# Two of the three gathered tiles of a PEER expert layer: rows of V gathered by token and summed by VectorE in PSUM, in place of TensorE products

## The chip, the cores and the metric

One core of one Trainium2 chip. The metric is device time in microseconds of one execution; the median of three runs of the kernel before is 3828.0 us (3827.8 to 3831.39).

## What is computed

One layer over 1024 tokens of width 1024: an attention and a long-convolution branch, then a PEER expert layer. For each token and each of 8 heads, product keys pick 16 of 16384 experts; expert e is one neuron with a row of U and a row of V. Only this last part bears on the change (cut from the reference):

```
best, pos = lax.top_k(cand, PEER_TOPK)
eidx = jnp.take_along_axis(cidx, pos, axis=-1)
g = jax.nn.softmax(best, axis=-1)
a = jnp.einsum('chkd,cd->chk', u_tab[eidx], xc)
wgt = (jax.nn.gelu(a.astype(jnp.float32)) * g).astype(xc.dtype)
return jnp.einsum('chk,chkd->cd', wgt, v_tab[eidx])
```

So every token has 128 experts, 128 weights, and its output is the weighted sum of 128 rows of V, 4 KB each.

## The kernel before

The 1024 tokens are 8 tiles of 128. Tiles 0 to 4 (`DT = 5`) go through **dense()**: it runs over all 128 blocks of 128 experts, whatever was picked. For each block it loads uT (`ur`) and V (`vr`), splits both into a high and a low part (`split`, lines 89 and 90: ScalarE copies, VectorE or, for half of the V blocks, GpSimd subtracts), forms the activations of 640 tokens with 48 matmuls of 320 columns (`mm3`, lines 84 to 86; gelu on ScalarE, line 1022), multiplies them with the gate weights on VectorE (line 982) and splits them again. After each chunk of four blocks (`CH = 4`), `products` multiplies them with V, 12 matmuls of 512 columns for each of 10 results, and VectorE adds each result to an accumulator in SBUF (line 1004). The PSUM pool of these results has five banks.

Tiles 5 to 7 (`E`) are **gathered**. `usweep` fetches, for each of the 128 experts of a token, the rows of U with a token per partition (an indirect DMA issued by GpSimd, line 886), and VectorE multiplies each with the token's vector and sums (line 887, with a second short instruction that reads the accumulator). `vsweep` fetches rows of V in another layout: an expert per partition (line 911, indices `eT`, transposed), one gather for 32 experts of 4 tokens at a time, as the order of the tokens wants it. TensorE sums over the partitions: eight matmuls of 32x512 for four gathers (line 915) with weights laid out on diagonals (`wdz`, lines 905 and 906), accumulated in PSUM (`acc`, two banks). All eight wait for the fourth gather. Both layouts fetch the same bytes: 128 gathers of 512 KB for a tile. In the profile each of these float32 matmuls is two records, so one step of four gathers is 16.

The buffers: `row`, 7 of 4 KB a partition (`RW`), shared by usweep's and vsweep's gathers; `vg`, 2 (`VB`), of which a step of vsweep takes one; and `h2`, one, in which usweep holds the tile's tokens.

What sets the order: `weave` runs dense() and takes steps of `background()` between its steps. background() runs usweep of tile 5; then usweep of tile 6 in turn with vsweep of tile 5; usweep of tile 7 in turn with vsweep of tile 6; then vsweep of tile 7. Each step is four gathers with what consumes them. From this a scheduler makes the order on each engine. Each engine then works in its order: an instruction that waits holds back all that stand behind it.

Of the kernel before, what the change touches and what calls it, by code (L numbers as in the profile page):

```python
# [10 lines left out]
F32 = mybir.dt.float32  # L11
# [4 lines left out]
OP = mybir.AluOpType  # L16
# [5 lines left out]
D = 1024  # L22
# [31 lines left out]
RW = 7  # L54
VB = 2
# [6 lines left out]
GB4, MGB4, OA4, OB4 = 2, 2, 1, 3  # L62
ND, DC = 2, 23
LR = 3
BGR = 1.3
DT = 5


def body(tc, d, out, dbg=None):
# [11 lines left out]
    V, S, G, PE, SY = nc.vector, nc.scalar, nc.gpsimd, nc.tensor, nc.sync  # L81
# [10 lines left out]
    with es:  # L92
# [194 lines left out]
        with ExitStack() as st:  # L287
# [15 lines left out]
            with ExitStack() as s2:  # L303
                p = pool("xp", 1, stack=s2)
# [111 lines left out]
            p = pool("zp", 2, stack=sz_, side="right")  # L416
# [164 lines left out]
            p = pool("zg", 2, stack=st, side="right")  # L581
# [314 lines left out]
        def vsweep(i, tops, ws, p, gp, ms, ap, res, wdz):  # L896
            w, eT = ws[i], tops[i][2]
            pt = ms.tile([128, 512], F32, name="ms")
            PE.transpose(pt[:, :128], w, ident)
            acc = ap.tile([128, 2, 512], F32, name="acc")  # L900
            pv = pt[:, :128].rearrange("p (c t) -> p c t", c=4)
            wT = res.tile([128, 4, 32], F32, name="wT", bufs=1)
            V.tensor_copy(wT, pv)
            for th in range(8):
                V.memset(wdz, 0.0)
                V.tensor_copy(wdz[:, :, th * 4:128:33], wT[:, :, th * 4:th * 4 + 4])
                for tm in range(4):
                    tl = th * 4 + tm
                    vgs = [gp.tile([128, D], F32, name="row", bufs=RW) if c else p.tile([128, D], F32, name="vg", bufs=VB) for c in range(4)]
                    for c in range(4):  # L910
                        G.indirect_dma_start(out=vgs[c], out_offset=None, in_=d["v"], in_offset=bass.IndirectOffsetOnAxis(ap=eT[:, c * 32 + tl:c * 32 + tl + 1], axis=0))  # L911
                    lead = None
                    for h in range(2):
                        for c in (3, 0, 1, 2):
                            mm = PE.matmul(acc[c * 32:c * 32 + 32, h, :], wdz[:, c, tm * 32:tm * 32 + 32], vgs[c][:, h * 512:(h + 1) * 512],  # L915
                                           start=tl == 0, stop=tl == 31, tile_position=(0, c * 32))
                            if lead is None:
                                lead = mm
                            else:
                                tc.add_manual_dep(mm.ins, lead.ins.name, mybir.DependencyInfo(mybir.DependencyClass.NoSync, mybir.DependencyReason.DATA), reason="behind the last gather")  # L920
                    yield 1
            gt = [gp.tile([128, D], F32, name="row", bufs=RW) for _ in range(4)]
            gates(gt)
            final(i, acc.rearrange("p a b -> p (a b)"), gt[2], gt[3], gt, p)


        def gbuild(i, i1T, i2T, gT, p, ms, on_act, gb, ob=False):
            for g in range(4):
# [121 lines left out]
        def gates(gt):  # L1050
            SY.dma_start(gt[0], modd[3:4, :].to_broadcast([128, D]))
            SY.dma_start(gt[1], d["fin_g"].to_broadcast([128, D]))
# [41 lines left out]
        E = list(range(DT, 8))  # L1094
        tops, ws = {}, {}
        with ExitStack() as sg:
# [19 lines left out]
            with ExitStack() as sk:  # L1116
                tkv = pool("tkv", 1, stack=sk)
                ra, rb = [], []
                sa_.close()
                sr_ = ExitStack()  # L1120
                rps = pool("rps", RB, PSUM, stack=sr_)
                rwp = pool("rw", 2, stack=sr_)
                for _ in rest(0, 4, rps, rwp, tkv, ra, hq):
                    pass
                v16, i16, hTh, hTl = ra
                ms = pool("ms", 1, PSUM, stack=sg, side="right")
                def weights_of(tiles, v16, i16, pools, on_act, gb):
                    bp, mg, tk, st_ = pools
                    for i in tiles:
                        for _ in topk(i, v16[:, i % 4], i16[:, i % 4], tk, bp, ms, True):  # L1130
                            pass
                        if i == DT - 1:
                            st_.close()
                        yield 1
                        yield from gbuild(i, *tops[i], bp, mg, on_act, gb, i < 4)

                def pools(stack, i, mgb):
                    st_ = stack.enter_context(ExitStack())
                    return (pool(f"gb{i}", 1, stack=stack, side="right"), pool(f"mg{i}", mgb, PSUM, stack=stack, side="right"),
                            pool(f"tk{i}", 1, stack=st_, side="right"), st_)  # L1140

                with ExitStack() as sb:
                    pl = pools(sb, 0, MGB)
                    rg = rest(4, 4, rps, rwp, tkv, rb, keep=(hTh[:, :, 512:], hTl[:, :, 512:]))
                    for _ in range(RB0):
                        next(rg)
                    for _ in weave(rg, weights_of(DD[:4], v16, i16, pl, OA, GB), RBR):
                        pass
                    pl[3].close()
                sr_.close()  # L1150
                v16, i16, _, _ = rb
                with ExitStack() as sb:
                    for _ in weights_of(DD[4:], v16, i16, pools(sb, 4, MGB4), OA4, GB4):
                        pass
                gp = pool("gp", 1, stack=sg, side="right")
                sl = ExitStack()
                tk = pool("tk2", 1, stack=sl, side="right")
                us = [usweep(i, tops, ws, gp, None, res) for i in E]

                def background():  # L1160
                    def tk_(i):
                        return topk(i, v16[:, i % 4], i16[:, i % 4], tk, res, ms, False)

                    yield from tk_(E[0])
                    for i in E[1:]:
                        yield from alternate(tk_(i), first(us[0], 24))
                    sl.close()
                    vp = pool("vp", 1, stack=sg, side="right")
                    ap = pool("ap", 1, PSUM, stack=sg, side="right")
                    wdz = vp.tile([128, 4, 128], F32, name="wdz")  # L1170
                    vs = [vsweep(i, tops, ws, vp, gp, ms, ap, res, wdz) for i in E]
                    yield from us[0]
                    for j in range(len(E) - 1):
                        yield from alternate(us[j + 1], vs[j])
                    yield from vs[-1]

                left = weave(dense(hTh, hTl, gp), background(), BGR)
                for _ in left:
                    pass
# [101 lines left out]
```

## Time and profile before

| | |
|---|---|
| median of three runs | 3828.0 us |
| the profiled execution | 3827.45 us |
| its span, first to last instruction | 3825.7 us |
| PE busy | 3526.5 us (92%) |
| VectorE (DVE) busy | 2449.8 us (64%) |
| ScalarE (ACT) busy | 1449.6 us (38%) |
| GpSimd (POOL) busy | 1672.5 us (44%) |
| mean granted TensorE clock | 0.958 of 2.4 GHz |

Times in the trace are microseconds from the span's start. The dense part begins at about 1700 us. Gathers of U run from 1865 to 3259 us, gathers of V from 1947 to 3540 us. VectorE's last step for tile 5 (line 1058) is at 2725.9 us, for tile 7 at 3554.1 us. A busy engine isn't always the one that holds the others up; the waits tell that, and PE's matmuls overlap in their records, so that a PE at 100% may still wait a little.

### The profile page before, as it was taken

Reading aid. Unit: us, or ns where it says so; the run is one execution under the profiler, and the core shown is the slowest. Engines: PE = TensorE matmul, PEld = TensorE weight load, DVE = VectorE, ACT = ScalarE, POOL = GpSimd, SP = SyncE. Lnnn points to the kernel's source line nnn. Section 1 sums busy time; section 2 is a strip of 40 time slices with the busy share of each in tenths; the row PEclk is TensorE's granted clock in tenths of the full one; section 3 lists DMA queues with packets and bytes.
Section 4 is the critical chain, followed back from the end, with each engine's and each line's share of the span. In section 5 each row is a group of like instructions: output and inputs, shape, how many; then the busy total and the mean of one; then the engine's idle time right before and its main releaser. Section 6 shows DMA issues by size and latency. Waiting matters only on the chain. (4 is left out here: it accounts for less than half of the span.)

```text
span 3825.7 us, 56007 instructions
## 1 busy us (share of the span) xinstructions
PE 3526.5 (92%) x21140; PEld 2963.8 (77%) x21140; DVE 2449.8 (64%) x5095; ACT 1449.6 (38%) x2966; POOL 1672.5 (44%) x1360
## 2 busy tenths in 40 slices
PE   5898998789989786989798999999999999999998
PEld 3787987567878686878688878888887888777897
DVE  4656544664446999999888766666556666433445
ACT  5543422446564278976312221212221222212222
POOL 0232143221321664123677666666565666556110
PEclk6999999999999897999899999999999999999999
DMA  4554355763322334443688899999999998989532
GB/s 161 184 157 155 121 204 197 273 218 101 108 83 67 119 141 173 156 164 130 214 311 304 303 335 328 336 343 327 331 326 337 335 343 314 353 318 333 172 108 98
DMA packets 334251, 868.48 MB, mean 227 GB/s; under 512 B 31778, under 2 KB 145378, under 8 KB 324765
## 3 DMA queue, kind: packets, MB, share of 16 engines
q0 software_dynamic: 123904, 453.04, 32.9%
q1 hardware_dynamic: 210076, 411.87, 31.4%
q8 instruction: 166, 2.72, 0.3%
q14 instruction: 105, 0.85, 0.1%
HBM read 777.63 MB, written 87.18 MB: 226 GB/s over the span
## 5 line engine op out<-in xcount | busy, mean ns | idle before, releaser
L84 PE MATMUL mm<-h2Th,uh 128*128 128x320 f32 x2048 | 641.0, 313 | 29.1 <-ACT uh L89 18.0
L86 PE MATMUL mm<-h2Th,ul 128*128 128x320 f32 x2048 | 638.2, 313 | 7.5 <-DVE ul L90 7.4
L85 PE MATMUL mm<-h2Tl,uh 128*128 128x320 f32 x2048 | 640.0, 313 | 0.0
L887 DVE SCALAR_TENSOR_TENSOR row<-row,h 128x1024 f32<-128x1024 f32 x384 | 493.9, 1306 | 153.2 <-DMA row<-in_u,ei 130.0
L886 POOL DMA_INDIRECT row<-in_u,ei x384 | 472.7, 1231 | 180.1 <-issue 85.9
L84 PE MATMUL mm<-vh,wh 128*128 128x512 f32 x1280 | 495.0, 396 | 25.5 <-DVE acc L1004 15.1
L85 PE MATMUL mm<-vl,wh 128*128 128x512 f32 x1280 | 502.0, 393 | 2.9 <-POOL vl L90 2.8
L86 PE MATMUL mm<-vh,wl 128*128 128x512 f32 x1280 | 497.2, 394 | 5.4 <-DVE wl L90 5.4
L911 POOL DMA_INDIRECT row<-in_v,eT x288 | 347.1, 1205 | 343.2 <-PE acc L915 179.7
L84 PEld LDWEIGHTS mm<-h2Th,uh 128*128 128x128 f32 x2048 | 389.3, 190 | 49.9 <-ACT uh L89 19.0
L86 PEld LDWEIGHTS mm<-h2Th,ul 128*128 128x128 f32 x2048 | 388.3, 190 | 22.9 <-issue 12.6
L85 PEld LDWEIGHTS mm<-h2Tl,uh 128*128 128x128 f32 x2048 | 389.1, 190 | 18.2 <-issue 16.8
L1004 DVE TENSOR_TENSOR acc<-acc,mm 128x512 f32<-128x512 f32 x322 | 211.9, 683 | 275.3 <-PE mm L86 275.1
L89 ACT CAST vh<-vr 128x1024 fp32r<-128x1024 f32 x133 | 139.3, 1048 | 474.1 <-PE mm L86 299.9
L84 PEld LDWEIGHTS mm<-vh,wh 128*128 128x128 f32 x1280 | 242.4, 190 | 89.8 <-DVE acc L1004 19.7
L86 PEld LDWEIGHTS mm<-vh,wl 128*128 128x128 f32 x1280 | 242.0, 189 | 72.8 <-issue 15.9
L85 PEld LDWEIGHTS mm<-vl,wh 128*128 128x128 f32 x1280 | 242.6, 190 | 60.3 <-issue 7.5
L90 POOL TENSOR_TENSOR vl<-vr,vh 128x1024 fp32r<-128x1024 f32 x67 | 167.8, 2505 | 251.3 <-ACT vh L89 250.7
L90 DVE TENSOR_TENSOR ul<-ur,uh 128x1024 fp32r<-128x1024 f32 (+1 forms) x130 | 169.3, 1302 | 162.7 <-ACT uh L89 161.3
L1022 ACT ACTIVATE ga<-mm 128x320 f32<-128x320 f32 x256 | 110.2, 436 | 421.2 <-PE mm L86 298.8
L89 ACT CAST uh<-ur 128x1024 fp32r<-128x1024 f32 (+1 forms) x130 | 137.8, 1060 | 268.7 <-DMA ur<-in_uT 177.8
L89 ACT CAST wh<-ga 128x640 fp32r<-128x640 f32 (+2 forms) x136 | 94.7, 696 | 362.8 <-DVE ga L982 189.3
(363 smaller groups left out, 7934.6 us busy)
## 6 DMA issues: line engine op xcount, KB each, us to landing
vr<-in_v SPq DMA_DIRECT2D x133, 512.0 KB
ur<-in_uT SPq DMA_DIRECT2D x128, 512.0 KB
gd<-gst SPq DMA_DIRECT2D x40, 1024.0 KB
gt<-gd SPq DMA_DIRECT2D x32, 1024.0 KB
wt<-in_ada_w SPq DMA_DIRECT2D x12, 2048.0 KB
cfr<-in_cf POOLq DMA_DIRECT2D x32, 512.0 KB, 5.2
mt<-in_cf POOLq DMA_DIRECT2D x16, 1024.0 KB, 6.4
mt<-in_ci POOLq DMA_DIRECT2D x16, 1024.0 KB, 7.7
```

The source lines that it names most:

```text
L84: PE.matmul(ps, ah, bh, start=start, stop=False)
L85: PE.matmul(ps, ah, bl, start=False, stop=False)
L86: PE.matmul(ps, al, bh, start=False, stop=stop)
L89: S.copy(hi, src)
L90: (eng or V).tensor_tensor(lo, src, hi.bitcast(F32), OP.subtract)
L886: G.indirect_dma_start(out=ug, out_offset=None, in_=d["u"], in_offset=bass.IndirectOffsetOnAxis(ap=ei[:, s_:s_ + 1], axis=0))
L887: V.scalar_tensor_tensor(ug, ug, 1.0, h2, OP.mult, OP.mult, accum_out=a[:, s_:s_ + 1])
L911: G.indirect_dma_start(out=vgs[c], out_offset=None, in_=d["v"], in_offset=bass.IndirectOffsetOnAxis(ap=eT[:, c * 32 + tl:c * 32 + tl + 1], ...
L1004: V.tensor_tensor(acc[:, i, h, :], acc[:, i, h, :], po, OP.add)
L1022: S.activation(ga[:, ts_], pa[:, :NS], AF.Gelu_apprx_tanh)
```

## The change

For tiles 6 and 7 (`VD`), a new function `vrows` takes the place of `vsweep`. It gathers rows of V with a token per partition, as usweep does for U: gather s fetches expert s of all 128 tokens (indices `ei`, as they are). VectorE multiplies the gathered tile by the column s of the weights and adds it to `acc`, one instruction for each gather (the first writes, the other 127 add in place). `acc` is the same two banks of PSUM; the last step (line 1058 and those behind it) stays. Tile 5 keeps vsweep.

The buffers are others: of three gathers in a row the second takes `row` in tile 6 and the one `h2` in tile 7 (usweep is through by then), the first and the third take `vg`.

```diff
+VD = (6, 7)
...
+        def vrows(i, tops, ws, p, gp, ap):
+
+            w, ei = ws[i], tops[i][1]
+            acc = ap.tile([128, 2, 512], F32, name="acc").rearrange("p a b -> p (a b)")
+            for s_ in range(128):
+                row = gp.tile([128, D], F32, name="h2" if i == 7 else "row", bufs=1 if i == 7 else RW) if s_ % 3 == 1 else p.tile([128, D], F32, name="vg", bufs=VB)
+                G.indirect_dma_start(out=row, out_offset=None, in_=d["v"], in_offset=bass.IndirectOffsetOnAxis(ap=ei[:, s_:s_ + 1], axis=0))
+                if s_ == 0:
+                    V.tensor_scalar(acc, row, w[:, 0:1], None, OP.mult)
+                else:
+                    V.scalar_tensor_tensor(acc, row, w[:, s_:s_ + 1], acc, OP.mult, OP.add)
+                if s_ % 4 == 3:
+                    yield 1
+            gt = [gp.tile([128, D], F32, name="row", bufs=RW) for _ in range(4)]
+            gates(gt)
+            final(i, acc, gt[2], gt[3], gt, p)
...
-                    vs = [vsweep(i, tops, ws, vp, gp, ms, ap, res, wdz) for i in E]
+                    vs = [vsweep(i, tops, ws, vp, gp, ms, ap, res, wdz) for i in E if i not in VD]
+                    vs += [vrows(i, tops, ws, vp, gp, ap) for i in VD]
```

Up to the first sum of tile 6 the order on VectorE is the same as before. Behind it the scheduler sets every engine's order anew. Line numbers of the changed kernel are higher: by 1 up to `vsweep`, by 18 behind `vrows` (L1004 is L1022 there, L982 is L1000); the gather is L933, the sum L937.

On VectorE, in the products of a chunk while tile 7's rows of U (L887, reading `h`, the tile's tokens) are gathered; before:

```order
L1004 TENSOR_TENSOR acc<-acc,mm 128x512 x6
L887 SCALAR_TENSOR_TENSOR row,a<-row,h_21926 128x1024
L1004 TENSOR_TENSOR acc<-acc,mm 128x512
L887 SCALAR_TENSOR_TENSOR row,a<-row,h_21926 128x1024
L1004 TENSOR_TENSOR acc<-acc,mm 128x512
L887 SCALAR_TENSOR_TENSOR row,a<-row,h_21926 128x1024
L1004 TENSOR_TENSOR acc<-acc,mm 128x512
L887 SCALAR_TENSOR_TENSOR row,a<-row,h_21926 128x1024
L1004 TENSOR_TENSOR acc<-acc,mm 128x512
L887 SCALAR_TENSOR_TENSOR row,a<-row,h_21926 128x1024 x2
L90 TENSOR_TENSOR ul<-ur,uh 128x1024
```

The same place in the changed kernel, with tile 6's sums of V among them (L888 is the old L887):

```order
L1022 TENSOR_TENSOR acc<-acc,mm 128x512
L937 SCALAR_TENSOR_TENSOR acc<-vg,gw_18487,acc 128x1024
L1022 TENSOR_TENSOR acc<-acc,mm 128x512
L937 SCALAR_TENSOR_TENSOR acc<-vg,gw_18487,acc 128x1024
L937 SCALAR_TENSOR_TENSOR acc<-row,gw_18487,acc 128x1024
L888 SCALAR_TENSOR_TENSOR row,a<-row,h_21926 128x1024
L1022 TENSOR_TENSOR acc<-acc,mm 128x512
L888 SCALAR_TENSOR_TENSOR row,a<-row,h_21926 128x1024
L1022 TENSOR_TENSOR acc<-acc,mm 128x512
L888 SCALAR_TENSOR_TENSOR row,a<-row,h_21926 128x1024 x2
L1022 TENSOR_TENSOR acc<-acc,mm 128x512
L937 SCALAR_TENSOR_TENSOR acc<-vg,gw_18487,acc 128x1024 x2
```

Between two emptyings of a bank there stand now up to three sums, of two kinds, where one stood.

On VectorE, in the products of a chunk after the last row of U; before:

```order
L905 MEMSET wdz 128x512
L1004 TENSOR_TENSOR acc<-acc,mm 128x512
L906 COPY wdz<-wT 128x4x4
L1004 TENSOR_TENSOR acc<-acc,mm 128x512 x6
L90 TENSOR_TENSOR wl<-ga_31002,wh 128x128
L1004 TENSOR_TENSOR acc<-acc,mm 128x512
```

And in the changed kernel, in tile 7's sums (the `h_` are the one buffer h2):

```order
L1022 TENSOR_TENSOR acc<-acc,mm 128x512 x4
L937 SCALAR_TENSOR_TENSOR acc<-vg,gw_19626,acc 128x1024
L1022 TENSOR_TENSOR acc<-acc,mm 128x512
L937 SCALAR_TENSOR_TENSOR acc<-vg,gw_19626,acc 128x1024
L937 SCALAR_TENSOR_TENSOR acc<-h_24182,gw_19626,acc 128x1024
L1022 TENSOR_TENSOR acc<-acc,mm 128x512
L937 SCALAR_TENSOR_TENSOR acc<-vg,gw_19626,acc 128x1024
L1022 TENSOR_TENSOR acc<-acc,mm 128x512
L937 SCALAR_TENSOR_TENSOR acc<-vg,gw_19626,acc 128x1024
L937 SCALAR_TENSOR_TENSOR acc<-h_24191,gw_19626,acc 128x1024
L1022 TENSOR_TENSOR acc<-acc,mm 128x512
```

One or two sums, each behind its gather, stand now between two emptyings where there was next to nothing.

On GpSimd, at the gathers of tile 7; before:

```order
L911 DMA row<-in_v,eT_19637 128x1024
L911 DMA vg<-in_v,eT_19637 128x1024
L911 DMA row<-in_v,eT_19637 128x1024 x3
L90 TENSOR_TENSOR vl<-vr,vh 128x1024
L911 DMA vg<-in_v,eT_19637 128x1024
L911 DMA row<-in_v,eT_19637 128x1024 x3
```

And in the changed kernel:

```order
L933 DMA h_24760<-in_v,ei_19635 128x1024
L933 DMA vg<-in_v,ei_19635 128x1024 x2
L933 DMA h_24769<-in_v,ei_19635 128x1024
L91 TENSOR_TENSOR vl<-vr,vh 128x1024
L933 DMA vg<-in_v,ei_19635 128x1024 x2
L933 DMA h_24778<-in_v,ei_19635 128x1024
```

The gathers take turns on three buffers, and the splits of V stand between them as before.

## Rows read from the trace of the kernel before

**Rows 1.** The page, forty slices: busy tenths of an engine and granted TensorE clock.
```profile
PE   5898998789989786989798999999999999999998
DVE  4656544664446999999888766666556666433445
PEclk6999999999999897999899999999999999999999
```

**Rows 2.** Busy time by stretch: us, then each engine's busy us (instructions), clock, DMA.
```profile
core 0: us, PE busy (x) PEld busy (x) DVE busy (x) ACT busy (x) POOL busy (x), PEclk, DMA share, GB/s
2738.90:3387.90 649.00, 634.70 (x3731) 510.92 (x3730) 376.69 (x524) 142.56 (x200) 403.49 (x324) 0.99 0.93 334
3387.90:3766.80 378.90, 375.74 (x2187) 312.27 (x2187) 152.37 (x180) 96.67 (x136) 113.24 (x88) 1.00 0.60 208
3766.80:3825.70 58.90, 47.54 (x259) 42.49 (x257) 35.98 (x41) 15.45 (x29) 1.44 (x1) 0.94 0.34 116
1937.80:2197.40 259.60, 236.06 (x1273) 209.90 (x1272) 214.18 (x312) 56.35 (x83) 179.95 (x118) 0.95 0.87 307
3596.60:3766.80 170.20, 170.20 (x955) 155.35 (x955) 76.90 (x87) 48.62 (x70) 19.69 (x9) 1.00 0.35 108
```

**Rows 3.** ScalarE in order of time: second gelu of blocks 112, 116, 120, 124.
```profile
3596.56 0.42 ACT L1022 ACTIVATE ga<-mm 128x320 f32<-128x320 f32 x1
...
3653.31 0.43 ACT L1022 ACTIVATE ga<-mm 128x320 f32<-128x320 f32 x1
...
3710.07 0.43 ACT L1022 ACTIVATE ga<-mm 128x320 f32<-128x320 f32 x1
...
3766.83 0.43 ACT L1022 ACTIVATE ga<-mm 128x320 f32<-128x320 f32 x1
```

**Rows 4.** PE's groups, 2738.9:3387.9, then 3387.9:3766.8: busy us, mean ns, idle before.
```profile
L915 PE MATMUL acc<-row,wdz 128*32 128x512 f32 x528 | 84.7, 598 | 4.1 <-DMA row<-in_v,eT 4.1
L915 PE MATMUL acc<-vg,wdz 128*32 128x512 f32 x176 | 83.8, 598 | 0.0
...
L915 PE MATMUL acc<-row,wdz 128*32 128x512 f32 x240 | 38.5, 598 | 3.2 <-DMA row<-in_v,eT 3.2
L915 PE MATMUL acc<-vg,wdz 128*32 128x512 f32 x80 | 38.1, 598 | 0.0
```

**Rows 5.** VectorE's prices, by line: duration min/median/max in ns, first and last start.
```profile
L1058 DVE TENSOR_TENSOR row<-row,acc x3: 1221/1221/1222, 2725.9 to 3554.1; 128x1024 f32<-128x1024 f32 x3
L1064 DVE SCALAR_TENSOR_TENSOR row<-row,fss x3: 1283/1284/1286, 2734.4 to 3560.6; 128x1024 f32<-128x1024 f32 x3
L1004 DVE TENSOR_TENSOR acc<-acc,mm x322: 621/683/690, 1815.7 to 3814.6; 128x512 f32<-128x512 f32 x161
```

**Rows 6.** VectorE's groups at 1937.8:2197.4, with idle time before and its releaser.
```profile
L887 DVE SCALAR_TENSOR_TENSOR row<-row,h 128x1024 f32<-128x1024 f32 x105 | 140.2, 1361 | 10.3 <-DMA row<-in_u,ei 10.1
L1004 DVE TENSOR_TENSOR acc<-acc,mm 128x512 f32<-128x512 f32 x40 | 26.1, 681 | 11.1 <-PE mm L86 11.1
```

**Rows 7.** Single instructions in order of time: start us, us, what, idle before it.
```profile
2017.39 1.21 DVE L887 SCALAR_TENSOR_TENSOR row<-row,h 128x1024 f32<-128x1024 f32 x1
...
2017.44 1.98 POOL L886 DMA_INDIRECT row<-in_u,ei  x1 [0.30 <-issue]
...
2021.60 1.57 POOL L886 DMA_INDIRECT row<-in_u,ei  x1 [0.30 <-issue]
...
2955.81 0.09 DVE L887 DVE_READ_ACCUMULATOR row<-row,h 128x1 f32 x1
2956.17 0.93 POOL L911 DMA_INDIRECT row<-in_v,eT  x1 [4.59 <-DVE row L887]
...
3408.67 0.82 DVE L90 TENSOR_TENSOR wl<-ga,wh 128x640 fp32r<-128x640 f32 x1
...
3410.61 0.94 POOL L911 DMA_INDIRECT vg<-in_v,eT  x1 [0.30 <-issue]
```

**Rows 8.** V gathers, issue to landing: at 2637:2640 (three), 2721:3304, 3304:3562.
```profile
DMA to landing us min/median/max: 4.3/5.2/5.5
...
DMA to landing us min/median/max: 4.2/6.4/13.2
...
DMA to landing us min/median/max: 4.1/7.7/12.1
```

**Rows 9.** The page, costliest groups: GpSimd's splits of V, busy us, mean ns.
```profile
L90 POOL TENSOR_TENSOR vl<-vr,vh 128x1024 fp32r<-128x1024 f32 x67 | 167.8, 2505 | 251.3 <-ACT vh L89 250.7
```

**Rows 10.** VectorE's groups at 2713:3304, with idle time before and its releaser.
```profile
L887 DVE SCALAR_TENSOR_TENSOR row<-row,h 128x1024 f32<-128x1024 f32 x128 | 161.8, 1284 | 70.3 <-DMA row<-in_u,ei 70.1
...
L905 DVE MEMSET wdz<- 128x512 f32 x9 | 4.4, 485 | 1.9 <-PE acc L915 1.5
...
L906 DVE COPY wdz<-wT 128x16 f32<-128x16 f32 x9 | 2.0, 217 | 0.1
```

## The prediction

> **What bounds the kernel now.** I read the page's forty slices first, then three stretches, then single lines, then prices. In the second half of the span PE stands at 9 or 8 in nearly every slice at a granted clock of 9, and VectorE at 5 to 8 [rows 1]. The stretches: A runs from the gelu of block 63 (2738.9 us) to that of block 101 (3387.9 us), 38 blocks or 9.5 chunks of four; B from there to block 124 (3766.8 us), 23 blocks or 5.75 chunks; C is the last 58.9 us. PE is busy 634.70 of 649.00 us in A and 375.74 of 378.90 us in B [rows 2]. So PE sets the pace. Where no gathered tile runs beside it, one chunk takes 56.8 us: the gelu of block 112 starts at 3596.56, that of 116 at 3653.31, of 120 at 3710.07, of 124 at 3766.83 [rows 3].
>
> What the gathered tiles take of PE is in A 84.7 us for 704 recorded matmuls (44 groups of 16) and in B 38.5 us for 320 (20 groups) [rows 4]. That is 1.92 us a group, 123.2 us for the 64 groups of tiles 6 and 7.
>
> **What goes.** Those 64 groups, with their waits for gathers (4.1 us in A, 3.2 us in B [rows 4]). Everything lies on PE, which is the bound, so taken alone this is worth 123 us, and the two transposes of w and 16 clears of wdz with their copies go too (0.7 us of VectorE for each clear and copy [rows 10], 11 us in all). PE's own floor after the change is 649.0 - 84.7 = 564 us in A and 378.9 - 38.5 = 340 us in B; at 56.8 us a chunk it would be 540 and 327.
>
> **What comes.** 256 VectorE instructions of 128x1024, each reading a gathered row in SBUF and adding into PSUM. No row shows VectorE writing PSUM. Nearest rows: two tensors and no scalar, one of them in PSUM, 1221 ns (the final multiply, L1058); the same shape with a scalar from a column, all in SBUF, 1284 ns (L1064) [rows 5]. Lower end 1.22 us; upper end 1.37 us, two of the 683 ns halves that read PSUM in L1004 [rows 5], as if each bank were a pass of its own. I take 1.28, the row with the same operation. Sum: 128 x 1.28 = 164 us in A and about as much in B.
>
> VectorE carries 376.69 us in A now, 39.7 us a chunk [rows 2]. With 17.2 us more and 0.7 us less for wdz it needs 56.2 us a chunk: nearly PE's 56.8 us. In A three things would then be full at once: PE, VectorE, and the gathers, 256 of them (the built order has tile 7's u gathers and tile 6's v sums between the splits of block 63 and of block 101, where before they ended by block 96). VectorE works in order, and behind a sum that waits for its gather are queued the splits of u, the weighing, and the emptying of PE's banks (L1004); for these PE waits.
>
> The trace has such a stretch already: 1937.8 to 2197.4 us, four chunks in which tile 5's u rows alone are gathered, 105 of them, each consumed by VectorE. There a chunk takes 64.9 us, PE is busy 236.06 of 259.60 us at a clock of 0.95, VectorE 214.18 us [rows 2, 6]. Read in three ways it prices A: by the chunk, 9.5 x 64.9 = 617 us; by the gather, 259.6/105 = 2.47 us, times 256 = 633 us; by VectorE's share of 82.5%, 9.5 x 56.2/0.825 = 647 us. I take the middle, 633 us: **16 us less than now in A**. So of the 85 us that PE is freed of there, most is not got back, because VectorE and the gathers come in its place.
>
> In B only tile 7's sums are left, 128 for 23 blocks, so VectorE is no bound: it needs 25.6 us for a bare chunk (76.90/3 [rows 2]) and 22 sums x 1.28 = 28.5 us, 54 of 56.8. But the buffers are. Before, a gathered tile of V had seven row buffers and two vg. Now tile 7 has two vg and the one h2, used in turn, so gather s + 3 is issued only when sum s is done. One turn is: the sum, 1.28 us; release to issue, 0.27 us (VectorE ends at 2955.90, POOL starts at 2956.17 [rows 7]); issue to landing. For the last, rows give 5.2 us (three gathers after an idle POOL), 6.4 us (the v gathers in A) and 7.7 us (the crowded end before) [rows 7, 8]. The ring thus passes a row every 2.25, 2.65 or 3.08 us. In B some of the crowd is gone (no u gathers, three in flight at most), so I take the middle: 128 x 2.65 = 339 us. Behind and between the gathers on POOL stand splits of v (L90), 2.5 us each by the page's mean [rows 9], about 12 of them in B; half of that, 15 us, I let fall into the ring. B = 354 us, **25 us less than now**, and above PE's 340. Since the sums stand in VectorE's order between the ten L1004 of a chunk and before the next split of u, a late gather reaches PE as soon as its five banks are full.
>
> Stretch C has the same work but for tile 7's last sums and its final step (three 1.2 us instructions on VectorE); I leave it.
>
> **A port shared.** Beside VectorE's instructions with two SBUF inputs, L887 and those behind it, a gather's issue on POOL takes 1.57 to 1.98 us at 2017 to 2023 us; where VectorE has nothing after 3409.5, it takes 0.94 us [rows 7]. The Trainium skill says the same (GPSIMD Engine Reference, section Specifications: the SBUF interfaces are shared, with contention from VectorE instructions that have two SBUF inputs); by that rule the new sums, with one input in PSUM, would leave issues at 0.94 us, and without it the ring would be 0.2 us slower, B some 27 us longer. The trace agrees as far as two SBUF inputs go; no row shows the new form.
>
> **The sum.** Against the profiled execution, 3827.45 us (span 3825.7; the median of the runs is 3828.0, so the two can be used alike): 3827.45 - 16 - 25 = 3786 us.
>
> **Rivals.**
> *PE stays the bound.* VectorE and the gathers hide. For it: PE stays at 98% in A now, while the DMA engines carry 334 GB/s at a share of 0.93 [rows 2], about what A would then ask of them. A = 564, B = 340: 3827 - 124 = 3704 us; with all waits gone (540, 327) 3666. Against it: 56.2 us of VectorE in order in 56.8 us leaves nothing for a wait, and in the stretch of 26 gathers a chunk PE did lose 9%.
> *VectorE waits for gathers more than now (slower).* Between 2713.1 and 3304.4 VectorE idles 70.3 us before 128 u sums [rows 10]. If the 128 v sums wait as much, A carries 2 x 70.3/9.5 = 14.8 us a chunk on top of 56.2: 71 us, 675 in all, +26. With landings as crowded as now, 7.7 us, the ring passes a row every 3.08 us: B = 394 + 15 = 409, +30. Together 3883 us. It decides from about A = 649 and a ring of 2.85 us, that is a landing of 7.0 us. For it: VectorE is emptied of slack in A, and three buffers replace nine. Against it: the stretch of u rows alone shows only 10.3 us of such waits in 105 [rows 6].
> *The ring doesn't bind.* With the landings that three gathers had after an idle POOL, 5.2 us, the ring passes a row every 2.25 us, 288 us for 128, and with the 15 us still under PE's floor. B is then PE's 340 us and the time 3827 - 16 - 39 = 3772 us. The v gathers of A, with two or three in flight, land at a median of 6.4 us [rows 8], so I give this 10%, within the forecast's share. The Trainium skill bears on it (DMA: Bandwidth & Descriptors, Anatomy of one DMA — SWDGE (gpsimd) path): 2.0 us plus bytes/436e3, for 512 KB an estimate of 3.2 us. By that rule this case would be certain; the trace differs, with no v gather's landing under 4.1 us and medians twice the page's figure [rows 8].
> *No change.* A at 647 (by VectorE's share) and a ring near 2.8 us give back all; 3820 to 3835 us.
> That the sums don't replace the matmuls can be excluded: in the built order L915 stands 256 times instead of 768 and the new line 256 times.
>
> **How the numbers follow.** Forecast 3786 us, with A from 617 to 647 and B from 340 to 370: 3757 to 3816; widened to 3745 to 3820 by what I can't price, 58% (10% of it with the ring not binding). PE the bound, 3666 to 3745: 17%. No change: 7%. Slower, 3835 to 3883: 18%. A measurement of this kernel tells about 0.2% (8 us) from no change. So faster 0.75, same 0.07, slower 0.18. For 8 in 10, the range leaves out half of the PE-bound case at the bottom and half of the slow one at the top: 3715 to 3850.
>
> **What would show it.** In the changed profile: L915 at about a third of its 768 instructions; the new line at 1.28 us each; chunks of 65 to 68 us in A and about 62 us in B, against 56.8 if PE stays the bound; VectorE's idle time before the new sums in B put down to the gather; POOL's gathers of tile 7 released by VectorE, and their median landing near 6.4 us; issues near 0.94 us when a new sum runs beside them. Wrong from the start would be a sum well above 1.37 us, or landings under 5.5 us with B at 56.8 us a chunk.

## The result, and the profile after

The changed kernel takes 3766.4 us, median of four runs (3756.3 to 3771.8), against 3829.7 us (3827.8 to 3831.6) for the kernel before in the same comparison: a ratio of 0.983 [0.981, 0.985], 63 us less. The profiled execution has a span of 3770.0 us, 55.7 less than the 3825.7 of before, and is the slowest of the four; the readings by stretch go by it.

The page of the kernel after, busy time and instructions of each engine, then two of its rows of forty slices:

```profile
PE 3421.9 (91%) x20114; PEld 2947.5 (78%) x20114; DVE 2736.9 (73%) x5317; ACT 1445.7 (38%) x2966; POOL 1700.5 (45%) x1360
...
PE   5899999789999886989889999999999999999988
...
DVE  4555554674446899999898866566599898777776
```

PE has lost 105 us of recorded work and VectorE has gained 287. Beside [rows 1] the last quarter of VectorE's row has gone from 6 and 4 to 9, 8 and 7: that is where the sums stand. PE's row still reads 9 there, which shows how little a tenth tells.

The same three stretches as in [rows 2], set by the same gelus (blocks 63, 101 and 124), in the kernel after:

```profile
core 0: us, PE busy (x) PEld busy (x) DVE busy (x) ACT busy (x) POOL busy (x), PEclk, DMA share, GB/s
2737.60:3332.00 594.40, 560.73 (x3073) 503.94 (x3071) 528.78 (x640) 142.05 (x202) 376.76 (x280) 0.99 0.92 331
3332.00:3712.90 380.90, 346.62 (x1831) 305.90 (x1832) 288.43 (x291) 94.64 (x137) 170.60 (x132) 0.97 0.79 261
3712.90:3770.00 57.10, 45.79 (x247) 40.74 (x245) 35.01 (x41) 15.30 (x29) 0.47 (x1) 0.92 0.34 120
```

Up to block 63 nothing moved (2738.9 before, 2737.6 now). A went from 649.0 to 594.4 us, B from 378.9 to 380.9, C from 58.9 to 57.1. So the whole gain lies in A. In B 38.5 us of PE's matmuls are gone [rows 4], its busy time is 29 us less (375.74 to 346.62), and the stretch gained nothing. PE was idle 14 us in A and 3 in B before; now it is idle 34 in each.

VectorE's groups in A of the kernel after (busy us, mean ns, idle time before and its releaser), with PE's group that starts the products:

```profile
L888 DVE SCALAR_TENSOR_TENSOR row<-row,h 128x1024 f32<-128x1024 f32 x128 | 171.9, 1358 | 8.0 <-DMA row<-in_u,ei 7.4 <-issue 0.6
L937 DVE SCALAR_TENSOR_TENSOR acc<-vg,gw,acc 128x1024 f32<-128x1024 f32 x89 | 114.0, 1281 | 14.0 <-DMA vg<-in_v,ei 13.6
...
L937 DVE SCALAR_TENSOR_TENSOR acc<-row,gw,acc 128x1024 f32<-128x1024 f32 x43 | 55.2, 1283 | 0.4
```

```profile
L85 PE MATMUL mm<-vh,wh 128*128 128x512 f32 x400 | 154.0, 403 | 20.5 <-DVE acc L1022 10.3 <-ACT vh L90 9.8 <-ACT wh L90 0.5
```

A sum is 1.28 us. The 70.3 us that VectorE idled before the u sums [rows 10] are down to 8.0, and 14.4 have come before the v sums. Why they are down isn't shown. Before, GpSimd, which issues both kinds of gather in order, waited 83.3 us in A for TensorE to be through with rows of V, and gathers of u stood behind. That wait went with TensorE's part, but GpSimd now waits nearly as long in A for VectorE to be through with them (waits of before, then of after: us in total, times, longest):

```profile
POOL row L911 <- PE acc L915: 83.3, 29, 8.2
```

```profile
POOL vg L933 <- DVE acc L937: 73.4, 52, 10.2
```

VectorE's groups in B of the kernel after, same columns:

```profile
L937 DVE SCALAR_TENSOR_TENSOR acc<-vg,gw,acc 128x1024 f32<-128x1024 f32 x79 | 101.5, 1285 | 43.5 <-DMA vg<-in_v,ei 43.1
L937 DVE SCALAR_TENSOR_TENSOR acc<-h,gw,acc 128x1024 f32<-128x1024 f32 x40 | 51.4, 1286 | 14.7 <-DMA h<-in_v,ei 14.5
```

Here VectorE waits 57.6 us for rows before its sums. That reaches PE through VectorE's order: of PE's 34 us of idle time in B, 29 end with a split or an emptied bank of VectorE's (three of PE's groups in B of the kernel after):

```profile
L87 PE MATMUL mm<-h2Th,ul 128*128 128x320 f32 x358 | 113.1, 317 | 14.1 <-DVE ul L91 14.1
...
L85 PE MATMUL mm<-vh,wh 128*128 128x512 f32 x252 | 99.8, 402 | 11.0 <-DVE acc L1022 10.1 <-ACT wh L90 0.9
L87 PE MATMUL mm<-vh,wl 128*128 128x512 f32 x252 | 98.8, 400 | 4.7 <-DVE wl L91 4.7
```

The chunks follow: before, the last three of B took 56.8 us each [rows 3], since tile 7 was over at 3554 us; after, the sums last until 3677 us and no whole chunk of B is under 62. ScalarE in order of time, gelus of blocks 108 and 112 of the kernel after, 64.9 us apart:

```profile
3453.38 0.43 ACT L1040 ACTIVATE ga<-mm 128x320 f32<-128x320 f32 x1
...
3518.24 0.43 ACT L1040 ACTIVATE ga<-mm 128x320 f32<-128x320 f32 x1
```

What the sums of B wait for shows in two places. First VectorE in order of time (start, duration, what, idle before it):

```profile
3344.10 1.27 DVE L937 SCALAR_TENSOR_TENSOR acc<-h,gw,acc 128x1024 f32<-128x1024 f32 x1
3345.83 1.23 DVE L91 TENSOR_TENSOR vl<-vr,vh 128x1024 fp32r<-128x1024 f32 x1 [0.46 <-ACT vh L90]
3349.18 1.22 DVE L91 TENSOR_TENSOR ul<-ur,uh 128x1024 fp32r<-128x1024 f32 x1 [2.12 <-ACT uh L90]
3350.32 0.82 DVE L1000 TENSOR_TENSOR ga<-ga,gt 128x640 f32<-128x640 f32 x1
3351.06 1.28 DVE L937 SCALAR_TENSOR_TENSOR acc<-vg,gw,acc 128x1024 f32<-128x1024 f32 x1
```

The sum at 3351.06 waits for nothing when its turn comes: its row is there. But 7.0 us lie between it and the sum before, because two splits that wait for ScalarE stand ahead of it, and the buffers of the landed rows stay full as long. Then GpSimd, later:

```profile
3579.20 0.94 POOL L933 DMA_INDIRECT h<-in_v,ei  x1 [2.06 <-DVE acc L937]
3583.52 2.41 POOL L91 TENSOR_TENSOR vl<-vr,vh 128x1024 fp32r<-128x1024 f32 x1 [3.38 <-ACT vh L90]
3586.08 0.95 POOL L933 DMA_INDIRECT vg<-in_v,ei  x1
```

Here a split of V stands ahead of the next gather and waits 3.38 us for ScalarE's copy. So the turn of the ring is made of the landing and of places in two in-order queues. Tile 7's 127 in-place sums run from 3304.1 to 3676.2 us: one every 2.95 us, a turn of 8.9 us for three buffers. Where only single emptyings of banks stand between, from the sum at 3559.30 to that at 3572.12, six steps take 2.14 us each, a turn of 6.4 us.

### The profile page after: what moved, and what is told of

The parts are those of the page before. It is cut to its first block, busy times and chain, and to the rows that moved or that the text cites. A ratio compares the mean times of both kernels' runs of the same rounds, so it can differ in the third digit from the quotient of the medians.

```text
span 3770.0 us, 54265 instructions
## 1 busy us (share of the span) xinstructions
PE 3421.9 (91%) x20114; PEld 2947.5 (78%) x20114; DVE 2736.9 (73%) x5317; ACT 1445.7 (38%) x2966; POOL 1700.5 (45%) x1360
## 5 line engine op out<-in xcount | busy, mean ns | idle before, releaser
L888 DVE SCALAR_TENSOR_TENSOR row<-row,h 128x1024 f32<-128x1024 f32 x384 | 501.8, 1324 | 96.2 <-DMA row<-in_u,ei 71.2
L887 POOL DMA_INDIRECT row<-in_u,ei x384 | 485.4, 1264 | 191.3 <-issue 82.8
L933 POOL DMA_INDIRECT vg<-in_v,ei x170 | 204.2, 1201 | 216.5 <-DVE acc L937 162.0
L1022 DVE TENSOR_TENSOR acc<-acc,mm 128x512 f32<-128x512 f32 x322 | 210.2, 680 | 92.2 <-PE mm L87 85.7
L937 DVE SCALAR_TENSOR_TENSOR acc<-vg,gw,acc 128x1024 f32<-128x1024 f32 x168 | 215.5, 1283 | 57.5 <-DMA vg<-in_v,ei 56.7
```

The source lines that it names most:

```text
L887: G.indirect_dma_start(out=ug, out_offset=None, in_=d["u"], in_offset=bass.IndirectOffsetOnAxis(ap=ei[:, s_:s_ + 1], axis=0))
L888: V.scalar_tensor_tensor(ug, ug, 1.0, h2, OP.mult, OP.mult, accum_out=a[:, s_:s_ + 1])
L933: G.indirect_dma_start(out=row, out_offset=None, in_=d["v"], in_offset=bass.IndirectOffsetOnAxis(ap=ei[:, s_:s_ + 1], axis=0))
L937: V.scalar_tensor_tensor(acc, row, w[:, s_:s_ + 1], acc, OP.mult, OP.add)
L1022: V.tensor_tensor(acc[:, i, h, :], acc[:, i, h, :], po, OP.add)
```

## The experiments

All ratios are against the kernel before, run on the same chip. B is always blocks 101 to 124, A blocks 63 to 101.

**More buffers for tile 7.** Tile 7 uses the seven row buffers as well.

```diff
-row = gp.tile([128, D], F32, name="h2" if i == 7 else "row", bufs=1 if i == 7 else RW) if s_ % 3 == 1 else p.tile(..., name="vg", bufs=VB)
+row = gp.tile([128, D], F32, name="row", bufs=RW) if (s_ % 3 if i == 7 else s_ % 3 == 1) else p.tile(..., name="vg", bufs=VB)
```

> Tile 7's gathers take two of the vg buffers and the seven row buffers in place of vg and h2: nine buffers where there were three, nothing else. Ring theory (stretch B, blocks 101 to 124, now 381 us, is set by three buffers turning in 8.9 us): B falls towards PE's 340 us, to 345 to 370 us, and the time to 3730 to 3755 us. Rival, VectorE has no slack in B whatever the buffers (288 us busy in order, and waits for ScalarE and PE): B stays at 375 to 385 us and the time at 3760 to 3775 us.

Measured: 3763.7 us, 0.983 [0.981, 0.985], the same as the change; B 386.5 us. VectorE's groups in B, then PE's, then the window of B and of its first 214 us:

```profile
L937 DVE SCALAR_TENSOR_TENSOR acc<-row,gw,acc 128x1024 f32<-128x1024 f32 x80 | 102.8, 1285 | 1.0
L937 DVE SCALAR_TENSOR_TENSOR acc<-vg,gw,acc 128x1024 f32<-128x1024 f32 x40 | 51.3, 1284 | 2.8 <-DMA vg<-in_v,ei 2.5
```

```profile
L85 PE MATMUL mm<-vh,wh 128*128 128x512 f32 x252 | 94.4, 405 | 37.0 <-ACT vh L90 36.8
```

```profile
3315.30:3701.80 386.50, 346.06 (x1864) 309.71 (x1863) 288.98 (x293) 98.15 (x139) 162.21 (x128) 0.93 0.74 258
...
3315.30:3529.30 214.00, 175.04 (x909) 154.49 (x908) 177.62 (x175) 45.16 (x64) 118.32 (x100) 0.88 0.88 309
```

The waits for gathers are nearly gone: VectorE idles 3.8 us before the sums, where it waited 57.6. B is no shorter. With more buffers the sums stand closer, some 30 in a chunk, and are done soon after block 116. In that part the DMA engines are at 0.88, PE's clock falls to 0.88, and chunks take 63 to 79 us; behind it they take 58.9 and 56.8. What PE waits for there is a split of V, and ScalarE makes it late because it waited for uT first (ScalarE in order of time, then PE):

```profile
3356.83 1.04 ACT L90 CAST uh<-ur 128x1024 fp32r<-128x1024 f32 x1 [21.28 <-DMA ur<-in_uT]
3358.08 1.05 ACT L90 CAST vh<-vr 128x1024 fp32r<-128x1024 f32 x1 [0.21 <-DMA vr<-in_v]
```

```profile
3359.18 2.50 PE L85 MATMUL mm<-vh,wh 128*128 128x512 f32 x5 [15.14 <-ACT vh L90]
```

The same follows once more, 20.62 us of ScalarE and 16.89 of PE up to 3499.70; the two make 32 of PE's 36.8 us. The theory that the ring sets B falls: the wait is real, but taking it away uncovers another of the same size.

**Fewer buffers for tile 7.** Two vg alone.

```diff
-row = gp.tile([128, D], F32, name="h2" if i == 7 else "row", bufs=1 if i == 7 else RW) if s_ % 3 == 1 else p.tile(..., name="vg", bufs=VB)
+row = gp.tile([128, D], F32, name="row", bufs=RW) if i != 7 and s_ % 3 == 1 else p.tile(..., name="vg", bufs=VB)
```

> Tile 7's gathers take the two vg buffers alone, two where there were three. Ring theory: a turn stays 8.9 us and passes two rows, 4.5 us a row, so 128 sums take 570 us and the time grows by 150 to 200 us, to 3915 to 3965 us. Rival, VectorE's work sets B: 3760 to 3785 us, as now.

Measured: 3806.3 us, 0.993 [0.991, 0.996]. The windows of B and of the end, then VectorE's group in B:

```profile
3326.20:3704.70 378.50, 348.14 (x1842) 308.03 (x1841) 259.52 (x272) 88.60 (x130) 151.12 (x121) 0.97 0.75 240
3704.70:3806.00 101.30, 53.45 (x256) 45.34 (x255) 59.70 (x62) 19.53 (x35) 19.92 (x16) 0.75 0.49 166
```

```profile
L937 DVE SCALAR_TENSOR_TENSOR acc<-vg,gw,acc 128x1024 f32<-128x1024 f32 x106 | 136.5, 1288 | 102.1 <-DMA vg<-in_v,ei 101.6
```

In B a row passes every 3.6 us (106 in 378.5), a turn of 7.2 us where three buffers had 8.9: a turn isn't a constant that is shared out over the buffers, as I had expected. VectorE's waits nearly doubled and B stayed at 378.5; the chunks there took fewer sums (some 18), and the rest ran past the end of the dense part, which cost 44 us in the last stretch.

**Tile 7's sums without their gathers.** Three rows are gathered and read over again.

```diff
+if i != 7 or s_ < 3:
     row = ...
+    held = (held + [row])[-3:] if s_ else [row]
+else:
+    row = held[s_ % 3]
+if i != 7 or s_ < 3:
     G.indirect_dma_start(out=row, ...)
```

> Of tile 7's 128 gathers only the first three are made; the other 125 sums read those three buffers again, so that the sums and their place among VectorE's work stay and no sum waits for a row (the output of tile 7 is wrong by that). Ring theory: B at 330 to 350 us, the time at 3715 to 3740 us. Rival, the sums' own 164 us on VectorE set B: B stays at 375 to 385 us, the time at 3760 to 3775 us.

Measured: 3712.8 us, 0.970 [0.968, 0.971]. The window of B:

```profile
3316.10:3649.40 333.30, 331.60 (x1846) 301.17 (x1845) 286.76 (x291) 94.51 (x136) 38.32 (x16) 1.00 0.37 114
```

VectorE does the same 287 us of work, and B is at PE's floor, with chunks of 59.0 and then 56.8 us. In B the sums cost nothing by themselves; the gathers cost 48 us.

**Tile 7's gathers made, not waited for by each sum.** Every sum reads one held row; the gathers fill the three buffers as in the change.

```diff
 G.indirect_dma_start(out=row, ...)
+if i == 7:
+    if s_ == 0:
+        held = gp.tile([128, D], F32, name="row", bufs=RW)
+        G.indirect_dma_start(out=held, ..., in_offset=bass.IndirectOffsetOnAxis(ap=ei[:, 0:1], axis=0))
+    row = held
```

> Tile 7's 128 gathers are made as in the change, into the same three buffers, but no sum reads them: all 128 sums read one row that is gathered once more at the start (so tile 7's output is wrong). The transfers stay and VectorE's waits for them go. If VectorE's waits in order are what B loses: B at 330 to 345 us, the time at 3712 to 3730 us, as without the gathers. If the transfers themselves slow the dense loads: B at 365 to 385 us, the time at 3750 to 3775 us.

Measured: 3732.6 us, 0.974 [0.971, 0.977]. The window of B:

```profile
3327.30:3681.70 354.40, 340.21 (x1870) 305.25 (x1869) 300.81 (x295) 96.44 (x138) 161.93 (x129) 1.00 0.81 277
```

The DMA engines carry as much as in the change, and B is 354.4 us. So of the 48 us over the floor some 27 are the sums' waits for their rows, and some 21 are there with the transfers alone. By whole times it is 34 and 20 us, from comparisons on different chips. The division is rough. The gathers go out closer here, one every 2.6 us (123 of them from 3299.4 to 3614.3) where the change has 2.95, and 24 more of PE's matmuls lie in this window than in the one without gathers. PE is idle for 14.2 us of it, most of that before VectorE has emptied a bank (PE's group that starts the products):

```profile
L85 PE MATMUL mm<-vh,wh 128*128 128x512 f32 x252 | 96.0, 395 | 11.5 <-DVE acc L1027 8.7 <-ACT vh L90 2.0 <-ACT ga L1045 0.8
```

**Tile 6 alone.** Tile 7 goes back to TensorE.

```diff
-VD = (6, 7)
+VD = (6,)
...
-vs = [vsweep(...) for i in E if i not in VD]
-vs += [vrows(...) for i in VD]
+vs = [vrows(...) if i in VD else vsweep(...) for i in E]
```

> Only tile 6 is summed by VectorE; tile 7 keeps the TensorE products. My theory, that all the gain is in stretch A and the two forms cost the same in B (381 against 379 us): 3758 to 3778 us, within 0.3% of the change. Rival, tile 7's sums bring a gain too, of some 25 us as forecast: 3785 to 3800 us.

Measured: 3786.0 us, 0.990 [0.987, 0.993]; A 586.3, B 402.4 us. Tile 6 is worth about 40 us and tile 7 about 20. I had looked for nothing from tile 7, since B doesn't shrink from before to after. The step I missed is that before, 12 of tile 7's 32 groups lay in A. With tile 6's sums in A, 29 of the 32 fall into B (TensorE's products of tile 7 there):

```profile
3312.10:3714.50 402.40, 57.51 (x464) 12.28 (x464) 0.99 0.69 243
```

That is 19 us more than the 38.5 of before [rows 4], and 378.9 + 19 is 398 of the 402.4. Against that B the change gains 21.5.

**All three tiles.** Tile 5 by sums as well.

```diff
-VD = (6, 7)
+VD = (5, 6, 7)
```

> Tile 5 is summed by VectorE as well, in the buffers that tile 6 has. My theory, that in a stretch with one kind of u rows and one of v rows most of what PE is freed of comes back: the chunks of tile 5's stretch (2185 to 2725 us, 64 us each, 8.4 of them) fall to about 59.5 us as those of A did, and the time to 3725 to 3740 us. Rival, that the sums only fit where VectorE and the transfers had slack: within 8 us of the change, 3758 to 3774 us.

Measured: 3743.4 us (3736.5 to 3753.9), 0.978 [0.975, 0.981], the fastest that computes the whole result; its interval touches that of the change at the end, its four runs lie all below the change's four. From block 28 to block 60 it takes 477.0 us where the change has 516.0; A is 598.8 and B 382.6.

**Tile 6's sums without their gathers.** The same edit as for tile 7, with `i != 6`.

```diff
+if i != 6 or s_ < 3:
     row = ...
```

> Of tile 6's 128 gathers only the first three are made; the other 125 sums read those buffers again (tile 6's output is wrong). VectorE's work and order in A stay. If the transfers (share 0.92 in A) are what keeps A at 594 us: A falls to 545 to 570 us, the time to 3715 to 3742 us. If VectorE's 89% in order keeps it: A at 585 to 600 us, the time at 3757 to 3775 us.

Measured: 3816.7 us, 0.997 [0.995, 0.999]; A 667.5 us. A miss: with no gather to wait for, the scheduler made another order. Three chunks now hold 115 of tile 7's 128 products with rows of U and 45 sums of V, and the four behind them 97 sums of V, with 24 gathers. The windows of the three chunks and of the four:

```profile
2771.20:3034.40 263.20, 196.83 (x936) 167.67 (x935) 253.38 (x349) 42.51 (x62) 169.36 (x117) 0.86 0.84 293
```

```profile
3034.40:3260.00 225.60, 225.60 (x1278) 206.79 (x1277) 206.85 (x198) 60.16 (x87) 46.20 (x32) 1.00 0.50 162
```

The three take 85 to 90 us each with VectorE at 96%, and PE's clock is 0.86 there: where the order is dense enough, VectorE holds PE up (PE waits 19.9 us for the low part of the weights from VectorE and 19.8 for the high part, which ScalarE copies behind it). The four take 55.4 to 57.9, and PE never stops, though VectorE is busy 92% of the time (206.85/225.60). So a VectorE as full as in A doesn't hold PE up by itself, where few rows are gathered and the DMA engines are at 0.50.

**Tile 7's sums in SBUF.** The accumulator is h2 instead of PSUM; the second gather of three takes a row buffer.

```diff
-acc = ap.tile([128, 2, 512], F32, name="acc").rearrange("p a b -> p (a b)")
+acc = gp.tile([128, D], F32, name="h2", bufs=1) if i == 7 else ap.tile([128, 2, 512], F32, name="acc").rearrange("p a b -> p (a b)")
```

> Tile 7's accumulator lies in SBUF (the buffer h2; the second of three gathers goes into a row buffer for it) in place of PSUM, so that its sums have two SBUF inputs. If the shared port holds as in the stretch of u rows: gathers of tile 7 are issued in a median of 1.2 to 1.6 us in place of 0.94, B grows by 10 to 30 us, the time to 3775 to 3797 us; the sums themselves stay at 1.28 us. Rival, the place of the accumulator doesn't matter: 3758 to 3774 us.

Measured: 3771.9 us, 0.983 [0.980, 0.986]; B 393.2 us. GpSimd's gathers (min, median, max ns) in this kernel, then in the change:

```profile
L933 POOL DMA_INDIRECT vg<-in_v,ei x71: 936/1279/1882, 3361.1 to 3674.4; - x71
```

```profile
L933 POOL DMA_INDIRECT vg<-in_v,ei x77: 935/940/1870, 3334.8 to 3663.3; - x77
```

And VectorE's sums in this kernel's B:

```profile
L937 DVE SCALAR_TENSOR_TENSOR h<-vg,gw,h 128x1024 f32<-128x1024 f32 x80 | 124.0, 1550 | 53.7 <-DMA vg<-in_v,ei 53.4
```

With two SBUF inputs both sides pay, but not in the same place. The median issue of these gathers goes from 0.94 to 1.28 us. The sum's mean goes from 1.285 to 1.55, and its median doesn't (1.284): twelve sums take 2.7 to 4.0 us, and each of them runs beside one of GpSimd's splits of V; beside the issue of a gather none takes more than 1.29. One of the twelve, VectorE then GpSimd:

```profile
3366.47 3.85 DVE L937 SCALAR_TENSOR_TENSOR h<-vg,gw,h 128x1024 f32<-128x1024 f32 x1
```

```profile
3366.80 2.42 POOL L91 TENSOR_TENSOR vl<-vr,vh 128x1024 fp32r<-128x1024 f32 x1
```

In the change none of the 254 sums takes more than 1.291 us, splits beside them or not. The rule of the Trainium skill (GPSIMD Engine Reference, section Specifications), that GpSimd shares its SBUF interfaces with VectorE and that VectorE's instructions with two SBUF inputs contend with it, agrees with both. In time it is lost among the waits: the ratio is that of the change.

**Half of VectorE's work for tile 6.** Its sums take 512 columns.

```diff
+m = 512 if i == 6 else D
-V.scalar_tensor_tensor(acc, row, w[:, s_:s_ + 1], acc, OP.mult, OP.add)
+V.scalar_tensor_tensor(acc[:, :m], row[:, :m], w[:, s_:s_ + 1], acc[:, :m], OP.mult, OP.add)
```

> Tile 6's sums (all but the first) take 512 of the 1024 columns, so that each costs VectorE some 0.75 us in place of 1.28 and A some 68 us less of VectorE's time; the gathers, their buffers and the order of the work stay (the right half of tile 6's output is wrong). If VectorE's share (528.8 of 594.4 us in A) keeps A above PE's floor of 564 us: A at 560 to 578 us, the time at 3733 to 3752 us. If the transfers keep it: A at 588 to 598 us, the time at 3760 to 3775 us.

Measured: 3769.1 us, 0.984 [0.982, 0.986]. The window of A:

```profile
2718.30:3308.30 590.00, 565.31 (x3066) 509.86 (x3065) 465.31 (x640) 141.67 (x202) 373.13 (x280) 0.97 0.93 333
```

VectorE is 63 us less busy and A 4 us shorter. VectorE's load doesn't hold A. The 4 us are no gain that can be told from another order's: in the five kernels above that differ from the change in tile 7 alone, A is 578.9 to 586.1 us, all below the change's 594.4.

**A second buffer for uT.** In the change's A the longest wait of all is ScalarE's for uT, the first line of the view of waits (us in total, times, longest):

```profile
ACT uh L90 <- DMA ur<-in_uT: 115.8, 16, 20.7
```

Space for a second `ur` is there with six row buffers. Two kernels, both with `RW = 6`, with and without it, and a third with it and all three tiles:

```diff
-RW = 7
+RW = 6
...
-CH, WB, VH, GA, UR = 4, 4, 4, 1, 1
+CH, WB, VH, GA, UR = 4, 4, 4, 1, 2
```

> The change with two buffers for the blocks of uT in place of one, and six row buffers in place of seven to make room. ScalarE's wait for ur is the longest in A (115.8 us). If the dense loads that come late behind the gathers cost A and B what they lose: A and B shrink by 10 to 25 us each, the time to 3720 to 3750 us. Rival, the load only comes earlier and the gathers pay for it, or VectorE's order sets the pace: 3755 to 3775 us.

> The change with six row buffers in place of seven and one buffer for uT, the half of the edit before last that only made room. In that run A (blocks 63 to 101) took 565 us, PE's floor, and the chunks before block 24 lost 60 to 70 us. If the second uT buffer brought A to the floor and the missing row buffer cost the early chunks: A at 585 to 600 us here, the early loss stays, the time at 3815 to 3850 us. If the missing row buffer (fewer gathers in flight) freed A: A at 560 to 575 us, the time near 3816 us. If the second uT buffer cost the early chunks: no early loss here, 3760 to 3785 us.

> All three gathered tiles summed by VectorE, with two buffers for uT and six row buffers. If both gains add up: 3743 us (all three) less what the two buffers give alone, 3695 to 3730 us. If the second buffer gives nothing: 3735 to 3752 us.

Measured: with it 3816.2 us, 0.996 [0.993, 0.998]; without 3808.2 us, 0.993 [0.991, 0.995]; all three tiles with it 3770.7 us, 0.984 [0.981, 0.987]. The window of A with it, then without:

```profile
2807.70:3372.70 565.00, 550.53 (x3029) 496.31 (x3028) 512.48 (x617) 139.89 (x203) 354.99 (x265) 0.99 0.92 330
```

```profile
2763.30:3372.10 608.80, 569.02 (x3102) 509.49 (x3101) 529.29 (x642) 146.22 (x207) 374.96 (x283) 0.97 0.91 325
```

With two buffers for uT, A is 565.0 us, the 564 that PE's floor was put at. PE's group that needs uT's high part, in A of the kernel with it, then the groups of both parts in A of the change, show the wait gone:

```profile
L85 PE MATMUL mm<-h2Th,uh 128*128 128x320 f32 x613 | 189.9, 310 | 0.0
```

```profile
L85 PE MATMUL mm<-h2Th,uh 128*128 128x320 f32 x624 | 193.8, 311 | 10.1 <-ACT uh L90 10.1
...
L87 PE MATMUL mm<-h2Th,ul 128*128 128x320 f32 x625 | 191.9, 310 | 1.7 <-DVE ul L91 1.7
```

Of the 44 us between the two kernels, 25 are idle time of PE (39.8 to 14.5); the rest is busy time, with 73 fewer of its matmuls in the window. From block 60 to block 124, a stretch with the whole of A and B in it, the kernel with it takes 976.5 us, the one without 1011.9 and the change 1000.4: 35 and 24 us. With all three tiles there is no such gain. The wait for uT is gone there too, but A is 591.9 us, where all three tiles with one uT and seven row buffers had 598.8, and from block 60 to block 124 it is 1007.7 against 1005.8. PE waits for splits of V in its place (its group that starts the products, in A of all three tiles with it):

```profile
L85 PE MATMUL mm<-vh,wh 128*128 128x512 f32 x398 | 150.9, 400 | 27.6 <-ACT vh L90 18.9 <-DVE acc L1022 5.9 <-ACT ga L1040 1.5
```

None of it is kept: block 60 starts at 2778.8 us with it, at 2739.1 without, at 2712.5 in the change. The row buffer less costs 27 us before A, and the second uT another 40, for which these runs give no cause. All three tiles lose early by it as well: block 24 comes at 2166.7 us, against 2133.1 with one uT and seven row buffers.

## Why the prediction was right, and where it wasn't

The forecast was 3786 us, faster, and the time is 3766. Its two terms missed by more than their sum: A was to be 633 us and is 594, B was to be 354 and is 381. One error of 39 and one of 27, with opposite signs: that the total came within 20 us is in part luck.

- **What goes.** Right. PE's floor in B was put between 327 and 340; without gathers B is 333.3. In A the lowest measured is 565.0, with the second uT buffer, at the 564 of the floor.
- **A sum at 1.28 us.** Right: 1.281 to 1.286 by name of its row. VectorE in A is 528.78/9.5 = 55.7 us a chunk, forecast 56.2.
- **A priced by the stretch of u rows.** This is the step that failed. The stretch has as many gathers a chunk (105/4 = 26) as A has now (256/9.5 = 27), and took 64.9 us a chunk; A takes 594.4/9.5 = 62.6, and 55.8 to 63.3 a chunk as far as block 92. Of my three readings the one by the chunk (617) is the least wrong, and I took the one by the gather (633). Above all I put the whole price down to VectorE and its gathers without reading what ended PE's waits there. The rows of PE's groups in that stretch, before, say it:

```profile
L84 PE MATMUL mm<-h2Th,uh 128*128 128x320 f32 x259 | 82.0, 317 | 7.0 <-ACT uh L89 7.0
...
L86 PE MATMUL mm<-h2Th,ul 128*128 128x320 f32 x258 | 80.9, 317 | 6.0 <-DVE ul L90 5.9
```

Of PE's 23.5 us of idle time 13 stand before matmuls that need uT's two parts, and ScalarE waits there 73.9 us for uT to land. So a transfer of the dense part was late there, and I made its time a price of each gather and of VectorE's work. The sizes come out of these rows. PE is busy 59.0 us a chunk in both stretches (236.06/4 and 560.73/9.5), but it idles 5.9 us a chunk there and 3.5 in A. Over 9.5 chunks that is 22 us, which is what 617 is too high by; 19 of them are the waits for uT's parts (13.0/4 = 3.3 us a chunk there, 11.8/9.5 = 1.2 in A). The other 16 of the 39 us come from reading by the gather. uT is late beside gathers only, since with the same one buffer a chunk without them takes 56.8 us [rows 3]; so gathers have a part in it, but with 26 or 27 of them in a chunk the wait was 3.3 or 1.2 us, and why it is shorter in A isn't shown. The runs bear out that VectorE's work isn't the price: half of it for tile 6 is worth 4 us, and in the four chunks without tile 6's gathers VectorE at 92% didn't hold PE up. A second buffer for uT, between kernels alike in all else, is worth 44 us in A and 35 from block 60 to 124; with all three tiles it gave next to nothing.
- **PE stays the bound.** As a rival it had A = 564 and 3704 us. A is nearer to it than to my figure, and the argument against it, that 56.2 us of VectorE in 56.8 leave nothing for a wait, was wrong: VectorE is 89% busy (528.78/594.4) and PE still gets 94% (560.73/594.4); in the four chunks without tile 6's gathers it is 92%, and PE 100%.
- **B by the ring.** Right in the mechanism as far as it goes: the gathers do cost in B (no gathers, 333.3), VectorE's waits are put down to them, and they reach PE through VectorE's splits and emptied banks, as forecast. Too small was the ring. A landing of 6.4 us was to give a row every 2.65 us; a row passes every 2.95, and 128 x 0.30 is 38 us, where I let in 15. The landing isn't given for the change itself; its median is 5.9 us with the sums in SBUF and 6.8 where each sum doesn't wait, so 6.4 fits. What I left out of the turn is the sum's place on VectorE behind splits that wait for ScalarE, and the gather's place on GpSimd behind a split. Wrong was that the ring is all that holds B: with nine buffers B stayed at 386.5, because ScalarE then waited for uT, and 21 us remain when no sum waits for its own row. Neither was a term.
- **Slower by waits.** Its B was 409 with a ring at 3.08 us; the ring came close to that, and B came out as its 128 x 2.95 = 378 us without the 15 us on top. Its A (675) is excluded: the waits shrank.
- **The ring doesn't bind, 3772.** The nearest number and the wrong reason: its B was 340.
- **The port.** Right: beside the sums an issue takes 0.94 us (median of 77), and up to 1.87 or so beside VectorE's splits. The sums in SBUF give the other case.
- **C left out.** Right, 1.8 us.

**Still open.** How the transfers alone cost B 21 us: late uT is how they did it in the nine-buffer run, but where no sum waited for its row, PE waited most before emptied banks. Why a second uT buffer shortens A with two tiles and hardly with three. Why a second uT buffer costs 40 us before A. And whether a kernel that keeps seven row buffers, and takes a second uT only once tile 6 begins, would hold both gains; that was not tried.

## What to carry to other kernels

Before a stretch is used as a price, read in it what ended the bound engine's waits: if that is a transfer which the change doesn't touch, its time is no price for each piece of the work beside it. A ring of buffers turns at landing plus the consumer's and the issuer's place in their in-order queues, and more buffers may only pack the consumers closer and make another transfer late. And count a removed piece of work where it would stand without the change, not where it stood before.

## What the runs showed of the hardware that I had not expected

- VectorE accumulating a 128x1024 fp32 tile in place in two banks of PSUM takes 1.28 us (1273 to 1291 ns over 254 sums), no more than the same operation all in SBUF [rows 5].
- The same sum with its accumulator in SBUF takes 1.28 us as well (median), also beside the issue of a gather, but 2.7 to 4.0 us in the twelve cases where GpSimd ran a split beside it, which reads two tiles in SBUF. With the accumulator in PSUM, no sum took more than 1.291 us.
- PE's granted clock, a mean of its two levels of 2.4 and 1.2 GHz, fell to 0.88 and 0.86 over stretches where PE was busy 175 of 214 and 197 of 263 us, the first with waits of 15 and 17 us in it. It is 0.97 to 1.00 in A and B before and after, where PE is 91 to 99% busy, and 0.95 in the stretch of u rows, at 91% [rows 2]: a starved PE tends to pay twice.
